# Two small instructions moved ahead of the opening barrier of an interleaving copy kernel

## Chip, cores, metric

One core of one Trainium2 chip, the other cores idle. The metric is the device time of one execution in microseconds (us); the median of the runs is quoted.

## The reference

Two float32 arrays of 32 x 256 x 1024 are interleaved element by element into one of 32 x 256 x 2048. There is no arithmetic: 67.1 MB come in and 67.1 MB go out.

```python
result = np.zeros((batch, seq, dim * 2), dtype=np.float32)
result[..., 0::2] = x
result[..., 1::2] = y
```

## The kernel before

Loads of 4 MB (128 partitions, 32 KB each) are issued from SyncE, alternately of x and y. VectorE copies each half tile into the even and the odd places of an output tile, and ScalarE issues the store of that tile. The x, y and output tiles have two buffers each. Ahead of the loop stands a tiny write: 16 rows of 512 bytes of zeros go to the output, where the first stores overwrite them later.

```python
    zero = wpool.tile([16, 128], fp32, name="zero")
    nc.vector.memset(zero, 0.0)
    first = dataclasses.replace(of, offset=0, ap=[[2 * WL, 16], [1, 128]])
    nc.scalar.dma_start(out=first, in_=zero)
    # ... [cut]
        nc.sync.dma_start(out=xtile, in_=xs)
        nc.sync.dma_start(out=ytile, in_=ys)
        # ... [cut: for each half tile]
            nc.vector.tensor_copy(out=otile[:, 0::2], in_=xsub)
            nc.vector.tensor_copy(out=otile[:, 1::2], in_=ysub)
            nc.scalar.dma_start(out=os_, in_=otile)
```

The program opens with a barrier of all engines: each drains, reports, and waits for release. After the kernel is built, its instruction lists are edited: the first x load, which waits for nothing, is taken out of the body and put ahead of SyncE's drain, so that it is issued before the barrier. (The barrier at the end is shortened by another edit of this kind, the same in both kernels.)

## Time and profile before

| | before |
|---|---|
| time, median of 6 runs | 316.21 us (315.44 to 316.38) |
| span of the profiled run | 313.6 us |
| DMA queues, busy share of the 16 engines | 50.0% loads, 49.6% stores |
| VectorE busy | 23% |

The span runs from the first instruction to the last; the time is some 1.8 us longer. The page and the start of the kernel are shown in the prediction. Two more lines of the kernel before are needed later. The first is from the bandwidth by stretches (stretch, length, busy VectorE, busy GpSimd, clock, DMA share, GB/s), for the five microseconds around the first large store:

```profile
25.00:30.00 5.00, 1.44 (x1) 0.00 (x0) 1.00 0.93 347
```

The rate falls to 347 GB/s there, against 434 from 8 to 12 us. The second is from the view of the tile of zeros, the time from the issue of its write to its landing:

```profile
DMA to landing us min/median/max: 6.3/6.3/6.3
```

### The profile page before, as it was taken

The numbers are of one execution on the slowest core, as the hardware profiler recorded it, in microseconds if no ns is written. First come the engines' busy times: TensorE is split into PE (matmuls) and PEld (weight loads), VectorE is DVE, ScalarE is ACT, GpSimd is POOL, SyncE is SP. The second block draws the span as 40 slices with busy tenths as digits, with TensorE's granted clock in tenths as the row PEclk, the third lists the DMA queues.
The fourth block names the chain that finished last, engine by engine and source line by source line (L and its number), as shares of the span: only waits on it lengthen the run. The fifth ranks groups of instructions, "written<-read, shape, count | busy, mean of one in ns | idle before, by whom it ended". The sixth has DMA issues, their size and how long they took to land.

```text
span 313.6 us, 140 instructions
## 1 busy us (share of the span) xinstructions
DVE 72.8 (23%) x33; POOL 0.2 (0%) x4
## 2 busy tenths in 40 slices
DVE  0433002231022410325003150131501305023500
POOL 0000000000000000000000000000000000000000
DMA  8999999999999999999999999999999999999997
GB/s 344 460 405 397 464 405 464 405 464 405 460 410 447 422 439 431 435 435 426 443 410 460 401 468 401 468 401 464 405 464 405 464 405 460 410 447 422 439 431 334
DMA packets 4640, 134.23 MB, mean 428 GB/s; under 512 B 528, under 2 KB 544, under 8 KB 544
## 3 DMA queue, kind: packets, MB, share of 16 engines
q1 hardware_dynamic: 2304, 67.11, 50.0%
q10 hardware_dynamic: 2336, 67.12, 49.6%
HBM read 67.11 MB, written 67.12 MB: 428 GB/s over the span
## 4 chain that ended last, share of the span: by engine, by line
DMA 83%; DVE 11%; DVEq 1%; issue 0%
DMA out_dram<-otile 76%; DMA ytile<-in_y_dram 7%; DVE otile L72 6%; DVE otile L71 5%; DVEq L84 1%; DVEq L71 0%
## 5 line engine op out<-in xcount | busy, mean ns | idle before, releaser
L71 DVE COPY otile<-xtile 128x4096 f32<-128x4096 f32 x16 | 36.6, 2295 | 184.8 <-DMA out_dram<-otile 173.6
L72 DVE COPY otile<-ytile 128x4096 f32<-128x4096 f32 x16 | 36.6, 2292 | 39.8 <-DMA ytile<-in_y_dram 39.8
L46 DVE MEMSET zero<- 16x128 f32 x1 | 0.2, 165 | 0.9 <-PEq L134 0.9
L134 POOL MEMSET const-bfloat16-1.0<- 128x1 bf16 x1 | 0.1, 101 | 0.0
L134 POOL MEMSET const-uint8-127<- 128x1 uint8 x1 | 0.1, 101 | 0.0
L134 POOL MEMSET const-float32-0.0<- 128x1 f32 x1 | 0.1, 98 | 0.2 <-issue 0.2
L134 POOL MEMSET const-float32-1.0<- 128x1 f32 x1 | 0.1, 98 | 0.0
## 6 DMA issues: line engine op xcount, KB each, us to landing
out_dram<-otile ACTq DMA_DIRECT2D x16, 4096.0 KB, 29.1
xtile<-in_x_dram SPq DMA_DIRECT2D x8, 4096.0 KB, 43.6
ytile<-in_y_dram SPq DMA_DIRECT2D x8, 4096.0 KB, 60.7
out_dram<-zero ACTq DMA_DIRECT2D x1, 8.0 KB, 6.3
```

The lines of the kernel that those rows point to most:

```text
L46: nc.vector.memset(zero, 0.0)
L71: nc.vector.tensor_copy(out=otile[:, 0::2], in_=xsub)
L72: nc.vector.tensor_copy(out=otile[:, 1::2], in_=ysub)
L84: tc.compile()
L134: nc = _bacc.Bacc("TRN2", target_bir_lowering=False, num_devices=1)
```

## The change

The intent: what ScalarE's queue does first should be done as early as what SyncE's queue does first. The memset and the tiny write that waits for it are moved ahead of the barrier as well, by the same kind of edit. No instruction is added or removed.

```diff
+    for engine, opcode in (
+        (mybir.EngineType.SP, "DMACopy"),
+        (mybir.EngineType.DVE, "Memset"),
+        (mybir.EngineType.Activation, "DMACopy"),
+    ):
         # ... [cut: finds the first such instruction of the body]
-    assert not moved.sync_info.on_wait
+        waits = moved.sync_info.on_wait
+        assert not waits or engine == mybir.EngineType.Activation
         # ... [cut: a second check of the wait; takes it out, finds the engine's first Drain]
+        opening.insert(gate, moved)
```

More of the change, by code (lines that the diff above doesn't have):

```diff
@@ L87 @@
     blocks = nc.main_func.blocks
-    opening = blocks[0].instructions
-    at, moved = next(
-        (b, i)
-        for b in blocks[1:]
-        for i in b.instructions
-        if i.engine == mybir.EngineType.SP and i.opcode == "DMACopy"
-    )
-    assert not moved.sync_info.on_wait
-    body = at.instructions
-    body.remove(moved)
-    gate = next(
-        n
-        for n, i in enumerate(opening)
-        if i.engine == mybir.EngineType.SP and i.opcode == "Drain"
-    )
-    opening.insert(gate, moved)
-    at.instructions = body
-    blocks[0].instructions = opening
+    for engine, opcode in (
[3 more added lines that the diff above has]
+    ):
+        opening = blocks[0].instructions
+        at, moved = next(
+            (b, i)
+            for b in blocks[1:]
+            for i in b.instructions
+            if i.engine == engine and i.opcode == opcode
+        )
+        waits = moved.sync_info.on_wait
+        assert not waits or engine == mybir.EngineType.Activation
+        assert all(w.ant_name.startswith("DVE") and w.wait_value == 1 for w in waits)
+        body = at.instructions
+        body.remove(moved)
+        gate = next(
+            n
+            for n, i in enumerate(opening)
+            if i.engine == engine and i.opcode == "Drain"
+        )
+        opening.insert(gate, moved)
+        at.instructions = body
+        blocks[0].instructions = opening
     last = nc.main_func.blocks[-1]
```

## The prediction

> **What bounds the kernel now.** I read the views in this order: the page's busy slices and queues (which resource is full), the chain of waits (is that resource also the path), bandwidth by stretches (where it is not full), and the timeline of the first microseconds (where the change acts). First the page:
>
> ```profile
> span 313.6 us, 140 instructions
> ...
> DVE 72.8 (23%) x33; POOL 0.2 (0%) x4
> ...
> DMA  8999999999999999999999999999999999999997
> ...
> q1 hardware_dynamic: 2304, 67.11, 50.0%
> q10 hardware_dynamic: 2336, 67.12, 49.6%
> HBM read 67.11 MB, written 67.12 MB: 428 GB/s over the span
> ```
>
> The reader is to see that the two queues together (q1 carries the loads, q10 the stores) keep the 16 DMA engines busy for 50.0 + 49.6 = 99.6% of the span. VectorE works 23% of it. Only the first and the last of the 40 slices are under "9". A packet here is one 32 KB row, 2048 of them in each queue: a load packet costs 0.500 x 313.6 x 16 / 2048 = 1.225 us of one engine, a store packet 0.496 x 313.6 x 16 / 2048 = 1.215 us. Each engine has 128 of each: 156.8 + 155.5 = 312.3 us of work in a span of 313.6. So 1.3 us per engine is idle, and that is all the idle there is. Now the chain of waits, in its order of time:
>
> ```profile
> 0.71 0.07 issue
> 0.78 21.14 DMA ytile<-in_y_dram
> 21.92 0.02 issue
> 21.95 4.51 DVE otile L72 x2
> 26.45 0.02 issue
> 26.47 40.91 DMA out_dram<-otile
> ```
>
> The chain begins with the first y load, issued at 0.78 right after the opening barrier, and then walks from transfer to transfer. Its DVE pieces look like lost time, but by the page the engines have other transfers meanwhile. The trap for this change is the first piece: it seems to say that the end hangs on the moment when y is issued. The bandwidth by stretches (columns: stretch, its length, busy VectorE, busy GpSimd, clock, DMA share, GB/s) answers that:
>
> ```profile
> 0.00:1.00 1.00, 0.14 (x1) 0.20 (x4) 1.00 0.24 66
> 1.00:2.00 1.00, 0.03 (x1) 0.00 (x0) 1.00 1.55 426
> 2.00:3.00 1.00, 0.00 (x0) 0.00 (x0) 1.00 0.38 164
> 3.00:4.00 1.00, 0.00 (x0) 0.00 (x0) 1.00 0.91 393
> 4.00:8.00 4.00, 0.00 (x0) 0.00 (x0) 1.00 1.13 485
> 8.00:12.00 4.00, 0.00 (x0) 0.00 (x0) 1.00 1.01 434
> ...
> 312.00:313.60 1.60, 0.00 (x0) 0.00 (x0) 1.00 0.01 0
> ```
>
> (A share above 1 comes from how packets fall into short stretches.) Only two places are not full: the first three microseconds, and the last 1.6. The trace's records of single packets say the same more sharply. The sixteen engines start their first packet, all of x, between 0.99 and 2.18 us and end it between 2.80 and 3.39; those first packets take 1.2 to 2.2 us, soon afterwards every one takes 1.213. The engine that ends its first packet at 3.39 then has 255 packets of 1.213 us = 309.3 us, which makes 312.7; the last packet of the kernel ends at 312.70. There is no hole in the stream. The time is therefore: until the first packets are in (3.4) + 309.3 + tail (0.9) = 313.6.
>
> **What the Trainium skill says.** "DMA: Bandwidth & Descriptors", section "Where 436 GB/s comes from": sixteen ports of 32 bytes at 850 MHz give 435.2 GB/s. The trace agrees: 434 GB/s in the stretch from 8 to 12 us, and 16 x 32768 bytes / 1.213 us = 432. The same page, section "Issuing engines are not separate DMA queues": transfers started from different engines run on the same 16 DMA engines and interleave, so a second issuer only saves issue time. The trace agrees, as the shares of the two queues add to 99.6% and no more. "Perfetto Trace Analysis", section "DMA Instruction — HWDGE (DVE, Sync)": what is shown of an issue is the wait for the descriptor generator, the generating and the pushing of a semaphore, while moving the data is outside it. The trace agrees: the tiny write shows 0.42 us of issue and takes 6.3 to land. "DMA: Bandwidth & Descriptors", section "Queues, rings and completion order": an engine takes turns between its queues packet by packet. The trace fits it where the tiny packets lie between two whole packets of x.
>
> **The change part by part.** Nothing is removed and nothing added: the memset of 16x128 zeros, the 8 KB write of them and the first x load are the same instructions. Two of them move ahead of the barrier. The timeline of the start:
>
> ```profile
> 0.00 0.37 SPq L57 DMA_DIRECT2D xtile<-in_x_dram  x1
> 0.23 0.10 POOL L134 MEMSET const-float32-0.0<- 128x1 f32 x1 [0.23 <-issue]
> ...
> 0.78 0.33 SPq L58 DMA_DIRECT2D ytile<-in_y_dram  x1
> 0.86 0.17 DVE L46 MEMSET zero<- 16x128 f32 x1 [0.86 <-PEq L134]
> 1.06 0.42 ACTq L48 DMA_DIRECT2D out_dram<-zero  x1
> 1.16 0.42 SPq L57 DMA_DIRECT2D xtile<-in_x_dram  x1
> 1.63 0.51 SPq L58 DMA_DIRECT2D ytile<-in_y_dram  x1
> 12.23 4.50 DVE L71 COPY otile<-xtile 128x4096 f32<-128x4096 f32 x2 [11.20 <-DMA xtile<-in_x_dram]
> ```
>
> 1. The memset. VectorE and ScalarE reach the barrier at about 0.12 and 0.13 us (the start of their drains, line 134, in the trace) and wait for release at 0.70. The memset can start near 0.2 instead of 0.86 and end near 0.4. VectorE's next work is at 12.23, so this saves nothing.
>
> 2. The tiny write. ScalarE's issue comes some 0.03 us behind the memset as before (1.03 to 1.06), so near 0.4 instead of 1.06: about 0.65 earlier. ScalarE's next issue is at 24.3 us and waits for VectorE's interleaving, so this saves nothing either. The data: 16 packets of 512 B, one per engine, 27 ns each, plus a 9 ns semaphore write. If they are served before x's first packet rather than between x packets, at most 0.04 us leaves the full stream.
>
> 3. The barrier, which is the cost. Before, the last to arrive was SyncE, whose drain ended at 0.55, and y was issued 0.23 later. Now ScalarE arrives last: 0.40 + 0.42 issue + about 0.2 for its drain = 1.02 (its drain behind the last store took 0.15), and 0.23 more gives y at about 1.25, so some 0.45 later than 0.78. The three loads behind the barrier move back together. The DMA engines have 8 packets of x each until about 12 us (x lands at 12.2); y's packets lie behind them in the same queue. The delay has some 10 us of cover, twenty times its size, so it costs 0.
>
> 4. The sum: 0 to -0.04 from the tiny packets, 0 from the barrier, and an unknown of perhaps 0.3 us either way from the start-up, where the slow first packets end between 2.80 and 3.39: the descriptors of the tiny write will be generated beside the first load's rather than beside the second x load's.
>
> **The rivals.** (a) The chain read literally: the end hangs on the issue of y, so +0.45 us, span 314.0 and time 316.6. For it stands the chain's first piece; against it, the 434 GB/s until 12 us. (b) The hope of the change: ScalarE's queue gets started 0.65 us sooner and everything after it too: -0.65, time 315.5. Against it: that queue's next transfer is 23 us later. (c) The tiny write falls into the start-up and holds x's first packet on some engines, or on the contrary wakes them earlier: as the whole stream of 309.3 us hangs behind the slowest first packet, this is the only way in which the change reaches the end one for one. Size: the spread of the ends of first packets is 0.6 us, so +-0.6 at most, time 315.4 to 316.7. (d) A steady state of another rhythm, as the two queues interleave differently from a shifted start. Against it: packets take 1.213 us whatever the neighbours, and the engines are never without work between 3 and 312 us.
>
> **Range and chances.** The time includes about 1.8 us beyond the span (profiled run: 315.39 against 313.6). The three timed runs of before lie at 315.44, 316.17 and 316.24, so 0.8 us of scatter is there with no change; with the profiled run they are two low and two high. I set 315.9, between the two clusters and near the upper one, and 315.1 to 316.7 for that scatter with 0.3 us of start-up on each side. Faster by over 2% would need 6.3 us, while all that lies outside the 309.3 us of full packets is 4.3 us: 1%, for something I don't understand. Slower by over 2% would need a hole of 6 us in a stream with 10 us of cover: 1%. Within 2%: 98%.
>
> **What would show it.** Step 1: memset ahead of 0.5 us and VectorE's first copy still at 12.2. Step 2: the tiny write issued at 0.3 to 0.6. Step 3: y issued at 1.0 to 1.4, yet x landing at about 12.2 and y at about 21.9 as now, and 430 to 435 GB/s from 4 us on. Step 4: the last packet still ends some 309.3 us behind the slowest engine's first; if the span moves, the ends of the first packets must have moved by as much. Wrong would be: y landing later by the delay of its issue (rival a), a hole in the engines between 3 and 312 us, a packet that takes other than 1.213 us in the steady state, or a barrier held for many microseconds because ScalarE's drain waits for the write to land (6.3 us now) rather than for its issue; even that would still lie inside x's 12 us.

## The result

The changed kernel took 316.13 us (median of 6, 315.45 to 316.26), the kernel before 316.21 (median of 6, 315.44 to 316.38). The ratio is 0.9998, 95% interval 0.9984 to 1.0013. The change does nothing that these runs can see.

The page of the changed kernel:

```profile
span 314.4 us, 140 instructions
...
DMA  9999999999999999999999999999999999999997
...
q1 hardware_dynamic: 2304, 67.11, 50.0%
q10 hardware_dynamic: 2336, 67.12, 49.4%
```

The engines are as full as before. The span of this one execution is 0.8 us longer than the profiled one of before (313.6). The runs of both kernels scatter by that much, so the two profiles caught different ends of the same scatter, and the 0.8 us isn't the effect of the change. The timeline of its start:

```profile
0.00 0.37 SPq L57 DMA_DIRECT2D xtile<-in_x_dram  x1
0.16 0.17 DVE L46 MEMSET zero<- 16x128 f32 x1 [0.16 <-issue]
...
0.36 0.38 ACTq L48 DMA_DIRECT2D out_dram<-zero  x1
1.17 0.33 SPq L58 DMA_DIRECT2D ytile<-in_y_dram  x1
...
12.38 4.50 DVE L71 COPY otile<-xtile 128x4096 f32<-128x4096 f32 x2 [12.05 <-DMA xtile<-in_x_dram]
```

The memset begins at 0.16 instead of 0.86 and the tiny write is issued at 0.36 instead of 1.06. The barrier waits for ScalarE now, and y is issued at 1.17 instead of 0.78. The chain of waits (start, length, what) absorbs this at once:

```profile
1.17 20.91 DMA ytile<-in_y_dram
22.07 0.02 issue
22.09 4.51 DVE otile L72 x2
26.62 42.61 DMA out_dram<-otile
```

The piece of y that begins 0.39 us later is 0.23 us shorter (20.91 against 21.14); y lands 0.15 us later than in the profile of before, and the end of the slowest first packet of x moved by 0.17 too (3.56 against 3.39 us by the records of single packets). The store behind it takes longer (42.61 us against 40.91); that belongs to the scatter, which is taken up below. The tiny write gained nothing by its early issue:

```profile
DMA to landing us min/median/max: 7.1/7.1/7.1
```

It was issued 0.70 us earlier and needed 0.8 us longer. Last, the bandwidth by stretches:

```profile
0.00:1.00 1.00, 0.17 (x1) 0.20 (x4) 1.00 0.00 0
2.00:3.00 1.00, 0.00 (x0) 0.00 (x0) 1.00 0.46 197
4.00:8.00 4.00, 0.00 (x0) 0.00 (x0) 1.00 1.13 485
8.00:12.00 4.00, 0.00 (x0) 0.00 (x0) 1.00 0.99 426
...
25.00:30.00 5.00, 1.59 (x1) 0.00 (x0) 1.00 0.97 328
```

The start is filled as it was. The stretch of 25 to 30 us is low again, 328 GB/s against 347: the only place behind the start where the two profiles differ by much.

### The profile page after: what moved, and what is told of

It reads as the page before. It is cut to its first block, busy times and chain, and to the rows that moved or that the text cites. A ratio compares the mean times of both kernels' runs of the same rounds, so it can differ in the third digit from the quotient of the medians.

```text
span 314.4 us, 140 instructions
## 1 busy us (share of the span) xinstructions
DVE 72.8 (23%) x33; POOL 0.2 (0%) x4
## 4 chain that ended last, share of the span: by engine, by line
DMA 83%; DVE 11%; DVEq 1%; issue 0%
DMA out_dram<-otile 76%; DMA ytile<-in_y_dram 7%; DVE otile L72 6%; DVE otile L71 5%; DVEq L84 1%; DVEq L71 0%
```

## The experiments

My theory: the 16 DMA engines are full from the first x packet to the end, and both moved instructions, and the later y, have cover (the "stream theory" of the texts below). A "no effect" can also be two effects that cancel, or a path that happened not to be stretched far enough, so most experiments make the suspected term large. The main rival (a) is the chain read literally: the end hangs on the issue of y. All edits are to the changed kernel; "before" is always the kernel before, run in the same rounds on the same chip. All kernels told here that ran gave right results.

Some numbers below come from the trace's records of single DMA packets, not from a view. A record does not name its DMA engine, so the packets were put in order of time into sixteen rows, one for each engine, each packet behind the one of its row that had just ended. The "excess" of a packet is its time beyond the usual 1.213 us.

### How far can the barrier be held?

VectorE gets extra memsets ahead of the barrier, so that y is issued ever later. The tiny write still waits for the first memset alone.

```diff
     nc.vector.memset(zero, 0.0)
+    pad = wpool.tile([128, 2048], fp32, name="pad")
+    for _ in range(7):
+        nc.vector.memset(pad, 0.0)
     # ... [cut]
-        (mybir.EngineType.DVE, "Memset"),
+        *[(mybir.EngineType.DVE, "Memset")] * 8,
     # ... [cut]
-        assert not waits or engine == mybir.EngineType.Activation
-        assert all(w.ant_name.startswith("DVE") and w.wait_value == 1 for w in waits)
+        assert all(w.ant_name.startswith("DVE") for w in waits)
```

The other runs have 3, 5 or 15 in place of 7, and one more in the list. With seven memsets:

> The changed kernel with seven more memsets of 128x2048 on VectorE ahead of the barrier, so that it holds the barrier far longer. A memset is estimated at 1.15 us, half of the 2.29 of a 4096-wide copy, so y is issued near 9 us. Stream theory: x's packets keep the engines busy to 12.2 and about 1.0 us pass from an issue to its first packet, so 9 us is still inside the cover: 315.4 to 316.5, same as before. Rival a: y's delay of about 8 us appears whole, 324.

My estimate of a memset was too small: one took 1.76 us, and they started 2.26 apart, so y was issued at 16.29 instead of 9, outside the cover. The time was 322.38 us (322.03 to 322.84, 4 runs; ratio 1.0208, interval 1.0194 to 1.0222; means 322.41 against 315.90, +6.51). The stretches show where it went:

```profile
8.00:11.00 3.00, 2.51 (x2) 0.00 (x0) 1.00 0.94 404
11.00:12.00 1.00, 0.51 (x2) 0.00 (x0) 1.00 0.01 0
12.00:16.00 4.00, 3.51 (x2) 0.00 (x0) 1.00 0.00 0
16.00:18.00 2.00, 1.70 (x2) 0.00 (x0) 1.00 0.89 246
```

No packet starts from 11 to 16 us. By the records of single packets the engines stand idle for 5.87 us in the mean (each for 5.3 to 6.9), and the first packet of y then has an excess of 0.65 us in the mean: 6.52 together, against 6.51 measured. Rival a, with y issued 15.5 us later than in before, wanted +15.5. (The memsets also hold VectorE's first copy, to 16.32 instead of 12.23. The interleaving still waits for y, which lands at 28.37, and the hole with the slow first packets behind it accounts for the time.) So this miss of an estimate still separates the two theories.

Fifteen memsets were to go with it:

> The same with fifteen memsets: y is issued near 18 us, behind the end of x's packets at 12.2. Stream theory: the engines are empty from 12.2 until about 19, so the time grows by about 6.8 us (perhaps 0.7 more for a second slow first packet), to 322.5 to 324. Rival a: by 17 us, 333.

Its chain of memsets deadlocked in the opening.

With three memsets:

> Three extra memsets instead of seven; by the spacing of 2.26 us measured in the run with seven, the third ends at 6.98 and y is issued near 7.3 us, 6.5 later than in before and well inside x's packets, which end near 12. Stream theory: no hole, time 315.3 to 316.5. Rival a (the chain's first piece is the path): +6.5 us, 322.4.

y was issued at 7.25 us. The time was 315.76 us (315.68 to 316.55, 4 runs), ratio 1.0004, interval 0.9989 to 1.0020, so that at most some 0.6 us can have come from a delay of 6.47. The chain of waits of this run:

```profile
7.25 14.63 DMA ytile<-in_y_dram
21.88 0.02 issue
```

It begins with y again, 6.47 us later than in before, and y lands at 21.88, where it was 21.92. The length of this piece was queueing behind x, and it shrinks by as much as the issue is delayed.

With five memsets:

> Five extra memsets: the fifth ends at 11.50, y is issued near 11.8 us, and about 0.95 us pass from an issue to its first packet, so y's packets start at 12.7 where x's end at 11.7 to 12.0. Stream theory: a hole of 0.8 to 1.0 us, and slow first packets of y behind it as in the run with seven (0.5 to 0.9 us of excess): +1.3 to +1.9 us, 317.2 to 317.9. Rival a: +11 us, 327.

y was issued at 11.77 us. The time was 318.34 us (318.13 to 318.46, 4 runs), ratio 1.0081, interval 1.0066 to 1.0097; the means differ by 2.56, more than I expected. The hole was 0.9 to 2.1 us, 1.43 in the mean, as the engines start their first packet of y 0.95 to 1.7 us after the issue, and not all at 0.95; the slow first packets added 0.64, and some 0.3 us were lost near 49 us, where the engines slowed once more, for a reason that was not looked into. Together 2.4. Rival a wanted +11.0.

The three points, by issue of y: 7.25 costs nothing to be seen, 11.77 costs 2.56, 16.29 costs 6.51. Between the last two 4.52 us of later issue cost 3.95. So the cover ends some 10 us behind the start, and the changed kernel's 1.17 is far inside.

### One half of the change

```diff
-        (mybir.EngineType.Activation, "DMACopy"),
```

> Of the two moved instructions only the memset stays ahead of the barrier; the tiny write is issued behind it. Stream theory (the 16 DMA engines are full from the first x packet to the end, so an issue with cover costs nothing): y is issued again near 0.8 to 0.95 us instead of 1.17, and the time stays within 315.4 to 316.4, ratio to before 0.999 to 1.001. Rival a (the end hangs on the issue of y, and the change's two halves cancel: an earlier tiny write gains 0.4, a later y loses 0.4): this one is apart from the changed kernel and level with before, or 0.4 faster than the changed kernel.

y was issued at 0.77, the tiny write too. The time was 315.50 us (315.30 to 316.31, 5 runs), ratio 0.9996, interval 0.9982 to 1.0011. Level with before, as expected; that two effects of 0.4 us cancel in the change isn't excluded by this run alone, as the interval spans 0.9 us, but the run with three memsets left no room for a cost of y.

### The tiny write left out

```diff
-    wpool = ctx.enter_context(tc.tile_pool(name="wp", bufs=1))
-    zero = wpool.tile([16, 128], fp32, name="zero")
-    nc.vector.memset(zero, 0.0)
-    first = dataclasses.replace(of, offset=0, ap=[[2 * WL, 16], [1, 128]])
-    nc.scalar.dma_start(out=first, in_=zero)
     # ... [cut]
-        (mybir.EngineType.DVE, "Memset"),
-        (mybir.EngineType.Activation, "DMACopy"),
```

> Memset and tiny write are left out; every output is still written by the large stores, so the result is right. Stream theory: 16 x 36 ns of packets less, one per engine, -0.04 us, not to be seen: 315.3 to 316.4. A rival, that the tiny write is there to wake the way of the stores: in both traces the loads' packets take 1.3 to 2.8 us instead of 1.21 around 26 to 28 us, when the first large store starts (excess summed over the engines 10 us before, 17 us after); if the tiny write shortens this, the excess grows here, to 30 us summed or more, and the time by 1 us or more, to 317 or above.

The time was 316.17 us (316.08 to 316.24, 5 runs), ratio 1.0011, interval 0.9997 to 1.0025. The excess of the load packets around the first store was 13 us summed over the engines, between the 10 of before and the 17 of the changed kernel. So the rival that the tiny write shortens this loss, with 30 us summed and 317 us without it, failed. A smaller effect is not excluded: the interval reaches 0.25%, and all five runs lie above 316.0, where three of the nine of before beside them do. That was seen after the fact and not run again.

### The first x load put back

Behind the barrier together with the other two:

```diff
-        (mybir.EngineType.SP, "DMACopy"),
-        (mybir.EngineType.DVE, "Memset"),
-        (mybir.EngineType.Activation, "DMACopy"),
```

> The first x load too goes back behind the barrier, as do memset and tiny write. Here the start of the stream itself moves: with the barrier released at about 0.6 us x is issued at about 0.7, so the first packets end 0.6 to 0.7 later than in before (3.9 to 4.1 instead of 3.4) and, as there is no cover, the stream theory expects all of it in the time: 316.6 to 317.0 against 316.2, ratio 1.001 to 1.003. If only rival a's y counts (issued 0.4 later than in before at most), +0.4 or less.

x was issued at 0.73. The time was 316.17 us (315.99 to 316.46, 5 runs), ratio 1.0012, interval 1.0000 to 1.0025: the ratio is in the expected range, the absolute time is below it. The records are clearer than the time: the median of the sixteen DMA engines ends at 313.21 us instead of 312.38, so +0.83. The mean time grew by only 0.3, less than the 0.7 by which x was late, though the interval, 0 to 0.8 us, holds both. In this profile no engine trails behind the others (the latest ends at 313.29), as one does in three profiles of the table below; whether that explains the small growth of the five runs is not shown.

And alone, with memset and tiny write ahead:

```diff
-        (mybir.EngineType.SP, "DMACopy"),
```

> Memset and tiny write ahead of the barrier, the first x load behind it (issued near 1.0 to 1.2). Question one, the time: the stream starts later by as much as x is issued later, so +0.8 to +1.2 against before, 317.0 to 317.5. Question two, why the tiny packets start at 5.2 to 5.3 us in both traces though they were issued at 0.36 in the one and at 1.06 in the other: if their place is behind three x packets in the engines' work, they now go first, before x, at 1.0 to 2.0 us; if the first use of ScalarE's queue takes some 4 to 5 us by itself, they still start near 5.

x was issued at 1.17 and the time was 317.45 us (317.33 to 317.79, 5 runs), ratio 1.0052, interval 1.0038 to 1.0066. The means differ by 1.59, more than the 0.8 to 1.2 that I expected. In the profile the median engine ends 1.19 us later, as much as x was late, and one engine had a packet with 1.89 us of excess besides; that the other four runs had such a packet too is not shown. The second question has a clear answer, from the stretches and the view of the tile of zeros:

```profile
1.00:2.00 1.00, 0.00 (x0) 0.00 (x0) 1.00 0.04 8
```

```profile
DMA to landing us min/median/max: 1.4/1.4/1.4
```

With nothing ahead of them, the tiny packets start at 1.25 us, 0.89 behind their issue, and land 1.4 us after it. In the kernel before and in the changed one they start at 5.24 or later, always after three 32 KB packets of x on their engine, whether they were issued at 0.36 or at 1.06. So it is their place behind x that holds them back, and the early issue moved them by nothing.

### y ahead of the barrier too

```diff
         (mybir.EngineType.SP, "DMACopy"),
+        (mybir.EngineType.SP, "DMACopy"),
```

> On top of the change the first y load also goes ahead of the barrier: y issued near 0.4 to 0.5 us instead of 1.17. Stream theory: y lands near 22 as before, time 315.4 to 316.4, ratio 0.999 to 1.001. Rival a (the chain read literally): 0.7 us faster than the changed kernel, about 315.3, ratio 0.9975 or so.

y was issued at 0.42. The time was 315.48 us (315.27 to 315.64, 5 runs), ratio 0.9989, interval 0.9977 to 1.0002. Rival a's 0.9975 is just outside, and no effect just inside. Two variants asked whether it is y that does this:

```diff
+        (mybir.EngineType.SP, "DMACopy"),
-        (mybir.EngineType.DVE, "Memset"),
-        (mybir.EngineType.Activation, "DMACopy"),
```

> The first x and the first y load ahead of the barrier, memset and tiny write behind it. The run with y ahead as well as memset and tiny write had all five runs low (315.27 to 315.64), which may be luck. If y's early issue is what does it, this one is low too, five runs of 315.3 to 315.6; stream theory: no reason for it, runs scattered over 315.3 to 316.4 as in before.

315.62 us (315.39 to 315.83, 5 runs), ratio 0.9994, interval 0.9981 to 1.0006.

```diff
         (mybir.EngineType.SP, "DMACopy"),
+        (mybir.EngineType.SP, "DMACopy"),
+        (mybir.EngineType.SP, "DMACopy"),
+        (mybir.EngineType.SP, "DMACopy"),
```

> All of the first four loads ahead of the barrier, with memset and tiny write. Stream theory: x issued at 0.00 as ever, everything else has cover: 315.3 to 316.4. If a fuller queue at the start makes the scatter narrow and low, five runs of 315.3 to 315.6, ratio 0.998 to 0.999; that would be a version slightly ahead of both kernels.

315.64 us (315.46 to 315.87, 5 runs), ratio 0.9995, interval 0.9983 to 1.0008. Neither is as low as its "if" asked, and both have a narrow scatter. So a guess was put to the test, together with more runs of the change itself:

> The kernel with y ahead as well, once more, to test a guess made after the fact: in the three kernels with y ahead none of 15 runs lay above 315.9, while 9 of the 27 runs of before beside them lay above 316.0. If that is real, 5 of 5 here are at or below 315.9 and the profile shows no load packet near 27 us with more than 1.3 us of excess. If it was luck, one or two of five lie above 316.0.

315.41 us (315.36 to 315.63, 6 runs), ratio 0.9989, interval 0.9977 to 1.0001; the largest excess of a load packet near 27 us was 0.76 us. The guess came true.

> The changed kernel itself, beside before, for more runs of both on one chip. Stream theory: both scatter over 315.3 to 316.5, with a third to two thirds of the runs above 316.0, and the ratio is 0.999 to 1.001. If the later issue of y (1.17 against 0.78) makes the upper part of the scatter more frequent, this one has 4 or 5 of 5 above 316.0 and before at most a third.

315.76 us (315.51 to 316.33, 6 runs) against 315.94 (315.34 to 316.26, 11 runs), ratio 1.0000, interval 0.9988 to 1.0012. One of six runs lay above 316.0, and four of the eleven of before. The changed kernel's first six had four above. So its upper part is not more frequent than that of before: 5 of 12 against 8 of 17.

### What the scatter of 0.8 us is made of

Eight profiles of the runs above tell where an engine loses time. This table is from the records of single packets: the end of the sixteen engines' first packets, the largest excess of a load packet between 24 and 31 us, and the end of the engines' last packets.

```
kernel           span    first packets end   largest excess   last packet, median / latest engine
before           313.6   2.80 to 3.39        0.70             312.38 / 312.70
changed          314.4   2.82 to 3.56        1.60             312.73 / 313.43
changed again    313.9   2.79 to 3.52        1.20             312.71 / 313.04
memset only      314.3   2.76 to 3.39        1.73             312.47 / 313.42
no tiny write    314.3   2.83 to 3.37        1.43             312.50 / 313.37
three memsets    313.6   2.81 to 3.34        0.75             312.47 / 312.72
y ahead too      313.8   2.84 to 3.28        0.83             312.67 / 312.96
y ahead again    313.5   2.87 to 3.28        0.76             312.53 / 312.68
```

The first packets end at nearly the same time in all. The three long executions (314.3 and 314.4) are those in which one or two engines have a load packet with 1.4 us of excess or more, all of them at 27.2 to 27.5 us, shortly after the first large stores are issued (24.3 and 26.5 us). Each engine has a fixed number of packets, so what it loses there it never makes up: in two of the three this engine ends last, 0.9 us behind the median. In the changed kernel's profile two engines have such a packet (1.55 and 1.60 us), and they end 0.05 and 0.11 us ahead of the last, one that began late and lost 1.15 us in two packets. So in these profiles the long end of the scatter goes with the loss at the first store. The slow packets move with the issue of the first store: where a run issued it at 30.72 us (seven memsets), they start at 32.30 to 34.24. They are packets of loads, and in before they start at 26.12 to 27.74 (those with more than 0.4 us of excess), ahead of the first packet of any large store (29.07). The third load of y and the second store are issued at about the same time (26.47), so which of these issues does it is not separated. Why an engine gets such a packet in one execution and not in the next is open.

## Why the prediction was right, and where its working was not

The predicted 315.9, with 315.1 to 316.7 and 98% for "same", held: 316.13.

Step 1 held: memset from 0.16 to 0.33, first copy at 12.38. Step 2 held for the issue (0.36; "near 0.4") and failed for the packets: the 0.04 us was to come from their going before x, and they stayed behind three packets of x. It is far below what could be measured. Step 3 held: y at 1.17 where 1.25 was worked out, nothing lost, and the cover of about 10 us is now measured by the three held barriers instead of argued. Of its tests, "430 to 435 GB/s from 4 us on" holds in neither kernel (485 from 4 to 8 us, then 347 and 328 from 25 to 30); the prediction had overlooked that stretch in its own profile. Rivals a and b are refuted, a by the held barriers (0, 2.56 and 6.51 us where it wanted 6.5, 11.0 and 15.5), b by the tiny write that lands at the same time and by the run without it. Of rival c little can be seen: with x at 0.00 the slowest first packet ends at 3.28 to 3.56 us, with no pattern by the place of the tiny write (3.56 and 3.52 in the changed kernel, 3.34 in the run with three memsets, which has the tiny write at the same place, 3.39 in before). The two profiles of the changed kernel do have the latest of these ends; 0.17 us is below what the times can show.

The part that failed is "soon afterwards every one takes 1.213", with the sum built on it, step 4's test, and rival d's "1.213 us whatever the neighbours". "There is no hole in the stream" holds in so far as no engine stands idle from 25 to 30 us; what the proof missed is that its packets there take longer, up to 1.91 us in before and 2.81 in the changed kernel. The sum of 255 packets of 1.213 us came out at 312.70 by coincidence. In the records a packet follows its forerunner on its engine by 1.210 us, not 1.213, so 255 of them are 308.6 us; the missing 0.7 is what the latest engine lost between 25 and 30 us, where the load packets slow down shortly after the first store is issued. The engines lose 0.5 to 0.85 us there in the profile of before and 0.8 to 1.65 in that of the changed kernel. The corrected sum for an engine is: the end of its first packet, plus 308.6, plus its own loss at the first store. For the last engine of before it gives 3.39 + 308.6 + 0.69 = 312.68 (measured 312.70). In the changed kernel it gives 3.12 + 308.6 + 1.65 = 313.37 for the next to last (measured 313.39), and 3.56 + 308.6 + 1.15 = 313.31 for the last (measured 313.43), where 0.12 us stays unexplained. The test that the prediction set itself, "the last packet still ends some 309.3 us behind the slowest engine's first", failed accordingly: it was 309.9 in the changed kernel's profile; so did its sign of being wrong, "a packet that takes other than 1.213 us", come true. For the same reason the 0.3 us of unknown was put in the wrong place: the start-up moved by 0.17 us, while most of the 0.8 between the two profiles comes from 25 to 30 us. The range held because it was set from the scatter of the measured runs, whose origin it didn't need to know.

A version slightly ahead of both may be there: with the first y load ahead of the barrier none of 21 runs (four entries, three kernels) lay above 315.9 us, while 10 of 29 runs of before beside them lay above 316.0. (The expectation says 9 of 27, as it counts one set of nine runs twice; it is 6 of 18.) The gain in the mean is 0.05 to 0.11%, and each single interval reaches 1. In the one test made after the guess, six of six runs were at or below 315.9 and five of the eleven of before; luck alone would deal these runs so in some 4% of cases. The runs without the tiny write, five of five above 316.0 against three of nine, come out at some 3% by the same count. So both stay hints: the gain is not shown, and a mechanism is open; the profile of x and y ahead without the other two still has a load packet with 1.34 us of excess.

## What to carry to other kernels

Moving an instruction earlier pays only if something waits for it: look for who waits next, and when. A transfer in the chain of waits whose length is mostly queueing behind another transfer gives its slack back one for one (here 6.47 us later, 6.51 shorter), so before shortening the way to its issue, ask what the engines do meanwhile; delaying the issue on purpose measures that slack. When a sum from the profile comes out to the second decimal, check its terms separately: here a pitch that was 0.003 us too large hid a loss of 0.7 us.

## What the Trainium skill lacked or had wrong

- "DMA: Bandwidth & Descriptors", section "Latency and other measured facts", gives about 600 ns to the first byte for transfers issued from SyncE or ScalarE. Here the first packet started 0.89 us behind the issue of an 8 KB write on idle engines, and 0.99 to 2.18 us behind that of a 4 MB load, by engine. The records show starts of packets, which need not be the same thing as first bytes.
- The same page, section "Queues, rings and completion order", has the engine take turns between its queues packet by packet. It counts some 9 to 17 descriptors to a packet, so its packet need not be what the trace records as one. In the trace, three 32 KB packets of the first load went ahead of a 512-byte packet of the other queue on each engine, whether that was issued 0.36 or 1.06 us after the load's own issue; the first packet of a large store started 4.80 us behind its issue (24.27 and 29.07 us in before), behind packets of loads. The page has no number for such a wait.
- No page I read has the cost of the first packets of a stream: 1.2 to 2.2 us instead of 1.21 at the start, and 0.65 us of excess in the mean again when the engines had run empty (5.87 us idle) in the middle of the kernel.
- No page I read has the slowing of running loads when the first large stores are issued: 0.5 to 1.65 us per engine, in packets that start some 1.9 to 3.5 us behind the issue of the first store (24.27 and 26.12 to 27.74 us in the profile of before), ahead of that store's own first packet.
- "DMA: Bandwidth & Descriptors", section "Where 436 GB/s comes from", was right with its 435.2 GB/s: 433 to 434 GB/s of mixed loads and stores in the steady state (30 to 310 us), and 434 of loads alone (8 to 12 us, before). Its remark that for transfers between HBM and SBUF the HBM side, at some 358 GB/s, binds did not hold here, with the other cores idle.
